# A hybrid decoder layer on one core: another order of the weights' sums and roundings, adding DMAs spread over the taps, tiles kept on chip

## The chip, the core and the metric

The kernel runs on one core of a Trainium2 chip. The metric is the device time of one execution in microseconds (us); it computes one layer for 1024 prompt positions and 8 sample positions, in float32. Engines are named as in the profile: PE is TensorE (PEld its weight loads), DVE VectorE, ACT ScalarE, POOL GpSimd, SP SyncE, which here only issues DMAs.

## What is computed

```python
h = _rmsnorm(x, norm_g)
z = h @ w_in                                   # 1024 -> 6 x 1024
a_val, a_gl, a_gate, b_u, b_v, b_gate = split(z)
a_in = a_val * sigmoid(a_gl)
a_conv = depthwise_conv(concat([conv_buf, a_in]), conv_w) + conv_b     # 31 taps
a_out = silu(layernorm(a_conv, a_ln_g, a_ln_b)) * silu(a_gate)
gated = spatial_gate(layernorm(b_v, ...), w_s, b_s)    # 128x128 causal matrix per head
b_out = b_u * gated * silu(b_gate)
y = x + concat([a_out, b_out]) @ w_out
return rmsnorm(y, final_g), and the new convolution and chunk states
```

## The kernel before

Channels lie on partitions and the 1032 positions along the free dimension, so a [128, 1032] tile holds one block of 128 channels. The large product z = h @ w_in is done by a scheme of Strassen's kind with 7 products in place of 8, and each float32 factor is split into a rounded part and a rest, so that each product is 3 matmuls.

**Units and steps.** `units` is a list of 24 pairs of 128 output columns: P0 to P7 (value and its sigmoid gate, which feed the convolution), v0 to v3 (b_v), B0 to B7 (b_u and its gate), G0 to G3 (the gates of the convolution branch). Steps 0 and 1 do units 0 and 1 together, each step from 2 on does one unit. A step has 7 slots, one for each product of `PRODS`; a slot is 24 matmuls of 258 columns, a step 168. Within a slot the body calls work for the other engines between the two halves of its matmuls, and the order of these calls is the order on every engine's queue.

**Weights.** `wload` (L129) loads a unit's four quarters R1 to R4 from HBM, `wsum` (L140) makes the sums S1 to S4 of quarters on DVE, and `wsplit` (L145) rounds a sum on ACT (H, L154) and subtracts it on DVE (L, L155). Products use quarters 1, 2, 3 and 4 in this order: slots 0 and 1 need H1 and L1, slots 2 and 3 H2 and L2, 4 and 5 H3 and L3, 6 HL4. The order of the calls by slot is written in the loop (L844 to L872). Between slots 0 and 2 ACT copies the first sum of the products to another bank (`zb`, L885), and PE's slot 2 waits for that copy.

**Convolution.** For each P, `conv_items` (L320) puts taps into a queue `fill`: most taps are multiply-adds on DVE (`tap`, L336); the last GTS = 10 taps (none for P7) are products on ACT (`gtap`, L343), which two chains of DMAs issued by POOL add up in SBUF (`accum_op`, L351), and two more adding DMAs add the chains to the result (L365). `pump` (L99) takes items from `fill` for as long as the planner's estimate of DVE's time is less than 1 us ahead of its estimate of PE's.

**LayerNorm of the convolution** (`ln_items`, L371) stands in the same queue behind P7's taps: a mean (matmuls with ones), for each of the 8 blocks a load from DRAM (cD), a subtraction on DVE (`cen`, L398), a square on ACT, a store (ccD), a sum on DVE (`qacc`, L409); then the variance (`var`, L417), a broadcast of 1/std over PE (`ln_bc`, L437), and for each block a reload of ccD and of its gate (sgD), a multiplication (L462), Silu on ACT (L463), a multiplication with the gate (L468) and the split for the output product (`prep_m`, L626). The barrier `bar` holds this last part back until all 24 steps are issued.

**Output product.** 48 groups of 24 matmuls (`mmo`, L644): for each of three groups of positions first 8 output blocks over the gMLP half (half = 1), then 8 over the convolution half (half = 0). The weights of group s are split by `split_w` (L612) two groups ahead.

**Memory.** All of these tiles share one pool of NU = 51 buffers of 4 KB per partition. A new tile takes the buffer that a finished tile gave back and waits for the last instruction or DMA that used it. SP has one queue for all its loads and stores, and `later` delays a store by some slots.

## Time and profile before

| | |
|---|---|
| median of two runs | 878.38 us (878.18 to 878.57) |
| the profiled execution | 876.83 us |
| its span, first to last instruction | 875.0 us, so 1.83 us lie around it |
| mean granted clock of TensorE | 0.936 |
| busy: PE, DVE, ACT, POOL | 768.8, 646.6, 420.5, 82.4 us |
| start (before step 2 begins) | 0 to 97.7 us |
| steps 2 to 23 | 97.7 to 639.2 us |
| output product | 639.2 us to the end |

The digits of the page show tenths of busy time in 40 slices of 21.9 us. A row of the windows gives for one stretch its length, the busy time of each engine with its number of instructions, the granted clock, the DMA engines' share and GB/s. A row of the waits reads: who waited, for whom, us in total, how often, the longest.

### The profile page before, as it was taken

Reading aid. Unit: us, or ns where it says so; the run is one execution under the profiler, and the core shown is the slowest. Engines: PE = TensorE matmul, PEld = TensorE weight load, DVE = VectorE, ACT = ScalarE, POOL = GpSimd, SP = SyncE. Lnnn points to the kernel's source line nnn. Section 1 sums busy time; section 2 is a strip of 40 time slices with the busy share of each in tenths; the row PEclk is TensorE's granted clock in tenths of the full one; section 3 lists DMA queues with packets and bytes.
Section 4 is the critical chain, followed back from the end, with each engine's and each line's share of the span. In section 5 each row is a group of like instructions: output and inputs, shape, how many; then the busy total and the mean of one; then the engine's idle time right before and its main releaser. Section 6 shows DMA issues by size and latency. Waiting matters only on the chain. (4 is left out here: it accounts for less than half of the span.)

```text
span 875.0 us, 13987 instructions
## 1 busy us (share of the span) xinstructions
PE 768.8 (88%) x5648; PEld 751.0 (86%) x5648; DVE 646.6 (74%) x782; ACT 420.5 (48%) x568; POOL 82.4 (9%) x103
## 2 busy tenths in 40 slices
PE   6768998998879998997989999999879499999995
PEld 6767997988869997997989899998879489998994
DVE  4767996977657978878879889996854756725843
ACT  3443563555546575635747654334534434413431
POOL 1010011021130120120211201000010000000000
PEclk7779999999889998998998999999988789999998
DMA  8050178585695595795984977226879723573451
GB/s 297 0 171 16 50 178 202 147 180 148 163 203 178 144 239 149 169 213 153 181 227 97 229 182 200 85 74 230 291 293 413 281 73 121 170 264 105 146 209 51
DMA packets 67512, 151.48 MB, mean 173 GB/s; under 512 B 7448, under 2 KB 28632, under 8 KB 67432
## 3 DMA queue, kind: packets, MB, share of 16 engines
q1 hardware_dynamic: 55352, 106.50, 35.1%
q0 software_dynamic: 12096, 44.10, 26.0%
q8 instruction: 44, 0.72, 0.3%
q14 instruction: 20, 0.16, 0.1%
HBM read 83.58 MB, written 27.55 MB: 127 GB/s over the span
## 5 line engine op out<-in xcount | busy, mean ns | idle before, releaser
L650 PE MATMUL po<-mh,wh 128*128 128x384 f32 (+1 forms) x384 | 126.3, 329 | 19.0 <-ACT wh L616 11.7
L155 DVE TENSOR_TENSOR L<-R,H 128x1024 fp32r<-128x1024 f32 x72 | 87.8, 1220 | 72.0 <-ACT H L154 39.1
L650 PE MATMUL po<-ml,wh 128*128 128x384 f32 (+1 forms) x384 | 124.3, 324 | 0.6 <-DVE ml L641 0.6
L650 PE MATMUL po<-mh,wl 128*128 128x384 f32 (+1 forms) x384 | 124.3, 324 | 0.3 <-DVE wl L618 0.3
L154 ACT ACTIVATE H<-R 128x1024 fp32r<-128x1024 f32 x72 | 74.9, 1053 | 77.2 <-DVE R L142 39.9
L252 PE MATMUL zb<-hT,H 128*128 128x258 f32 x384 | 85.8, 307 | 29.3 <-ACT zb L885 21.4
L339 DVE SCALAR_TENSOR_TENSOR c<-apad,cw,c 128x1024 f32<-128x1024 f32 x85 | 108.6, 1278 | 2.4 <-ACT c L329 2.4
L339 DVE SCALAR_TENSOR_TENSOR accb<-apad,cw,accb 128x1024 f32<-128x1024 f32 x77 | 98.4, 1278 | 0.0
L650 PEld LDWEIGHTS po<-mh,wh 128*128 128x128 f32 x384 | 73.5, 191 | 23.0 <-ACT wh L616 12.0
L347 ACT ACTIVATE prod<-apad,cw 128x1024 f32<-128x1024 f32 x70 | 78.3, 1144 | 29.9 <-DMA prod<-prod 18.6
L252 PEld LDWEIGHTS zb<-hT,H 128*128 128x128 f32 x384 | 64.6, 206 | 32.1 <-ACT zb L885 22.7
L252 PE MATMUL zb<-hnB,HL 128*128 128x258 f32 x384 | 70.7, 299 | 15.1 <-DVE apad L286 11.9
L252 PE MATMUL zb<-lT,H 128*128 128x258 f32 x384 | 82.2, 297 | 0.8 <-DVE lT L238 0.8
L252 PE MATMUL zb<-hT,L 128*128 128x258 f32 x384 | 81.5, 295 | 0.0
L618 DVE TENSOR_TENSOR wl<-wr,wh 128x1024 fp32r<-128x1024 f32 x48 | 58.5, 1223 | 28.3 <-ACT wh L616 28.3
L252 PE MATMUL za<-lnB,H 128*128 128x258 f32 x384 | 77.3, 283 | 0.4 <-DVE lnB L222 0.4
L252 PE MATMUL za<-hnB,H 128*128 128x258 f32 x384 | 77.4, 283 | 0.0
L252 PE MATMUL za<-hnB,L 128*128 128x258 f32 x384 | 77.4, 283 | 0.0
L650 PEld LDWEIGHTS po<-mh,wl 128*128 128x128 f32 x384 | 73.3, 191 | 1.0 <-DVE wl L618 1.0
L650 PEld LDWEIGHTS po<-ml,wh 128*128 128x128 f32 x384 | 73.4, 191 | 0.8 <-DVE ml L641 0.8
L252 PEld LDWEIGHTS zb<-hnB,HL 128*128 128x128 f32 x384 | 58.3, 203 | 17.2 <-DVE apad L286 13.0
L351 POOL DMA_DIRECT2D prod<-prod x56 | 48.4, 864 | 208.3 <-ACT prod L347 109.7
(154 smaller groups left out, 1594.0 us busy)
## 6 DMA issues: line engine op xcount, KB each, us to landing
prod<-prod POOLq DMA_DIRECT2D x56, 512.0 KB, 6.0
R<-w_in SPq DMA_DIRECT2D x96, 256.0 KB, 4.8
wr<-w_out SPq DMA_DIRECT2D x48, 512.0 KB, 5.2
c<-prod POOLq DMA_DIRECT2D x14, 512.0 KB, 5.1
x<-xT SPq DMA_DIRECT2D x8, 516.0 KB, 5.6
sgD<-row SPq DMA_DIRECT2D x8, 516.0 KB, 3.3
mbD<-row SPq DMA_DIRECT2D x8, 516.0 KB, 2.9
ma<-ccD SPq DMA_DIRECT2D x8, 516.0 KB, 10.1
```

The costliest lines, as they stand in the source:

```text
L154: A.activation(h, r, AF.Copy)
L155: V.tensor_tensor(out=l, in0=r, in1=h, op=ALU.subtract)
L252: T.matmul(z[:, s, :PW], lhsT=HL[u, wi][we][:, wh, cs], rhs=F[name, p][xe][:, kt, :], start=first, stop=(kt == 3 and we == 1), skip_group_ ...
L339: V.scalar_tensor_tensor(out=o, in0=ap[:, j:j + NP_], scalar=cw[:, k, j:j + 1], in1=o, op0=ALU.mult, op1=ALU.add)
L347: A.activation(p, ap[:, j:j + NP_], AF.Copy, scale=cw[:, k, j:j + 1])
L351: G.dma_start(st["g", j % 2], p, accum_op=ALU.add)
L618: V.tensor_tensor(out=wl[s], in0=r, in1=wh[s], op=ALU.subtract)
L650: T.matmul(z, lhsT=w[:, cs], rhs=m_[g, half, kt][e], start=(half == 1 and kt == 0 and e == 0 and w is wh[s]), stop=(half == 0 and kt == KT ...
```

## The change

It is one edit in several parts. (1) A unit's R1 is loaded with R4 and R3 in slot 6, one slot earlier than before, and R2 in slot 1 in place of 3. The sums S1 and S3 go to slot 1, S2 to slot 2, S4 to slot 5 of the step before the unit's own; H3 and H4 move from slots 0 and 1 to slots 1 and 2 of its own. (2) GTS is 9 in place of 10, and these products come at every second tap. (3) In the start the squares of the second half of x are summed over blocks by matmuls, 48 in place of 12, and no longer by three additions on DVE. (4) Stores wait one or two slots longer. (5) `delay` items hold mean, variance and broadcast back by 3 to 4 us of estimated time. (6) The centred tiles of blocks 4 to 7 and the gates 6 and 7 stay in SBUF; their stores and reloads go. (7) A head's v is loaded in slot 0 in place of 2, and its normalisation is split between slot 6 and slot 1 of the next step.

```diff
@@ -26,9 +26,11 @@
 CW = 31
 H = CW - 1
 EPS = 1e-6
-GTS = (10,) * 7 + (0,)
+GTS = (9,) * 7 + (0,)
 NU = 51
 MMT = 0.12
+KEEP_C = (4, 5, 6, 7)
+KEEP_G = (6, 7)
 
 
 
@@ -104,6 +106,14 @@
                     return
                 fill.popleft()
                 continue
+            if kind == "delay":
+                if fn is None and margin < 1e8:
+                    fill[0] = (kind, cost, est["pe"] + cost)
+                    return
+                if margin < 1e8 and est["pe"] < fn:
+                    return
+                fill.popleft()
+                continue
             if kind == "pe" and not pe_ok:
                 return
             fill.popleft()
@@ -184,6 +194,13 @@
             for t in range(2):
                 T.matmul(ps[:CN, 0, c:c + 1], lhsT=sq[:, t, c // 3, CN * (c % 3):CN * (c % 3) + CN], rhs=ones_m[:, :1],
                          start=t == 0, stop=t == 1)
+
+    def stat_q(p, q, ps):
+        sq = xsq.pop((p, q))
+        for t in range(2):
+            for c in range(6):
+                T.matmul(ps[:CN, 0, c:c + 1], lhsT=sq[:, t, c // 3, CN * (c % 3):CN * (c % 3) + CN], rhs=ones_m[:, :1],
+                         start=q == 0 and t == 0 and c == 0, stop=q == 3 and t == 1, skip_group_check=True)
 
     def rstd_x(p, ps):
         V.tensor_scalar(out=xrs[:CN, p, :6], in0=ps[:CN, 0, :6], scalar1=EPS, scalar2=None, op0=ALU.add)
@@ -352,8 +369,8 @@
             return f
         for j in range(2, CW - gt):
             fill.append(("dve", 1.2, tap(j)))
-            if j < 2 + gt:
-                fill.append(("dve", 0.0, gtap(CW - gt + j - 2)))
+            if gt and j % 2 == 0 and j < 2 + 2 * gt:
+                fill.append(("dve", 0.0, gtap(CW - gt + j // 2 - 1)))
             if j == 10 and k:
                 acc_item(k - 1)
 
@@ -367,6 +384,7 @@
 
 
     ln = {}
+    mixa = {}
 
     def ln_items():
         acc_item(7)
@@ -388,6 +406,7 @@
             lnload(0)
             lnload(1)
             dve(2.0)
+        fill.append(("delay", 3.0, None))
         fill.append(("pe", 2.0, mean))
 
         def cen(k):
@@ -401,7 +420,10 @@
                 else:
                     ln["s", k] = U([128, NT], f"lns{k}")
                     A.activation(ln["s", k], c, AF.Square)
-                later(lambda: SP.dma_start(ccD[k], lnc.pop(k)), 1)
+                if k in KEEP_C:
+                    mixa[k] = c
+                else:
+                    later(lambda: SP.dma_start(ccD[k], lnc.pop(k)), 2)
             return f
 
         def qacc(k):
@@ -425,7 +447,9 @@
             G.tensor_tensor(out=rs[:, 1, :8], in0=rs[:, 0, :8], in1=nhalf[:, :8], op=ALU.pow)
             G.tensor_tensor(out=rs[:NS, 1, 8:9], in0=rs[:NS, 0, 8:9], in1=nhalf[:NS, :1], op=ALU.pow)
             ln["v"] = True
+        fill.append(("delay", 3.0, None))
         fill.append(("pe", 2.0, var))
+        fill.append(("delay", 4.0, None))
         fill.append(("bar", 0.0, None))
         fill.append(("pe", 2.5, ln_bc))
         for k in range(8):
@@ -448,15 +472,15 @@
         for k in range(3):
             mixa_load(k)
 
-    mixa = {}
-
     def mixa_load(k):
         while outq:
             slot_end()
-        mixa[k] = U([128, NT], f"ma{k}")
-        SP.dma_start(mixa[k], ccD[k])
-        ln["g", k] = U([128, NT], f"sg{k}")
-        SP.dma_start(ln["g", k], sgD[k])
+        if k not in KEEP_C:
+            mixa[k] = U([128, NT], f"ma{k}")
+            SP.dma_start(mixa[k], ccD[k])
+        if k not in KEEP_G:
+            ln["g", k] = U([128, NT], f"sg{k}")
+            SP.dma_start(ln["g", k], sgD[k])
 
     def mixa_norm(k):
         V.tensor_tensor(out=mixa[k], in0=mixa[k], in1=ln["r"], op=ALU.mult)
@@ -578,7 +602,7 @@
             V.memset(r1[:, :H], 0.0)
             V.tensor_tensor(out=r1[:, H:], in0=r1[:, H:], in1=r0, op=ALU.mult)
             dve(1.25)
-            later(lambda: SP.dma_start(csT[128 * k:128 * k + 128, :], r1[:, NP_:]), 1)
+            later(lambda: SP.dma_start(csT[128 * k:128 * k + 128, :], r1[:, NP_:]), 3)
             conv_items(k, r1)
             if k == 7:
                 ln_items()
@@ -589,10 +613,13 @@
             V.tensor_tensor(out=r1, in0=r1, in1=t2.pop(k), op=ALU.mult)
             V.tensor_tensor(out=r1, in0=r1, in1=r0, op=ALU.mult)
             dve(2.3)
-            later(lambda: SP.dma_start(mbD[k], r1), 1)
+            later(lambda: SP.dma_start(mbD[k], r1), 3)
             return []
-        later(lambda: SP.dma_start(sgD[2 * k], r0), 1)
-        later(lambda: SP.dma_start(sgD[2 * k + 1], r1), 1)
+        for e, r in enumerate((r0, r1)):
+            if 2 * k + e in KEEP_G:
+                ln["g", 2 * k + e] = r
+            else:
+                later(lambda e=e, r=r: SP.dma_start(sgD[2 * k + e], r), 2)
         return []
 
 
@@ -786,6 +813,8 @@
         scale_x(0, 3)
         xform(0, "nT3")
 
+        xst = []
+
         def start_x(si, slot):
 
             if si == 0:
@@ -795,22 +824,26 @@
                         wsum(u, "S2")
                         wsplit(u, 2)
                 if slot == 1:
+                    for q in range(2):
+                        square_x(1, q)
                     xform(0, "nB21")
-                    for q in range(4):
+                    for q in range(2, 4):
                         square_x(1, q)
+                    xst.append(PS("e", "xst1"))
                 if slot == 2:
+                    stat_q(1, 0, xst[0])
+                    stat_q(1, 1, xst[0])
                     xform(0, "T1")
                     for u in range(2):
                         wsplit(u, 3)
-                    sum_x(1)
                 if slot == 3:
+                    stat_q(1, 2, xst[0])
+                    stat_q(1, 3, xst[0])
+                    rstd_x(1, xst.pop())
                     xform(0, "nT4")
                     for u in range(2):
                         wsum(u, "S4")
                         wsplit(u, 4)
-                    p = PS("e", "xst1")
-                    stat_x(1, p)
-                    rstd_x(1, p)
                 if slot == 4:
                     bcast_x(1, PS("e", "xbc1"))
                     xform(0, "nB22")
@@ -846,29 +879,27 @@
                 if slot in (0, 1):
                     Z[bank] = PS(bank, f"z{bank}{si}")
 
-                if own and slot == 0:
-                    wsum(u, "S4")
+                if si and own and slot == 1:
                     wsplit(u, 3)
-                if own and slot == 1:
+                if si and own and slot == 2:
                     wsplit(u, 4)
                 if nxt is not None:
-                    if slot == 0:
-                        wload(nxt, 1)
-                    elif slot == 2:
+                    if slot == 1:
                         wsum(nxt, "S1")
-                    elif slot == 3:
                         wsum(nxt, "S3")
                         wload(nxt, 2)
+                    elif slot == 2:
+                        wsum(nxt, "S2")
                     elif slot == 4:
                         wsplit(nxt, 1)
                     elif slot == 5:
-                        wsum(nxt, "S2")
+                        wsum(nxt, "S4")
                     elif slot == 6:
                         wsplit(nxt, 2)
-                if slot == 6 and (own or si == 1) or (si == 0 and slot == 6):
+                if slot == 6:
                     n2 = 2 if si == 0 else u + 2 if own else 3
                     if n2 < N_U:
-                        for i in (4, 3):
+                        for i in (4, 3, 1):
                             wload(n2, i)
                 prod(slot, lanes, range(0, 2))
                 if slot == 0 and prev:
@@ -919,12 +950,13 @@
 
                 if own and si + 1 < len(steps) and units[u + 1][0] == "B":
                     h = units[u + 1][1]
-                    if slot == 2:
+                    if slot == (2 if h == 0 else 0):
                         v_load(h)
-                    if slot in (5, 6):
-                        v_norm(h, range(4 * (slot - 5), 4 * (slot - 5) + 4))
+                    if slot == 6:
+                        v_norm(h, range(0, 4))
                 if kind == "B" and own:
                     if slot == 1:
+                        v_norm(k, range(4, 8))
                         gw = gate_work(k)
                     if slot in (3, 4):
                         gw.pop(0)()
```

Three places show what the new order is. The first is ACT around the start of step 6 (unit 6): H6_1 to HL6_4 are the roundings of that unit's quarters, prod1 the products for the adding DMAs of P1, zb6 the copy that PE's slot 2 waits for. Before:

```order
L154 ACTIVATE H6_1_1772<-R6_1_1634 128x1024
L347 ACTIVATE prod1_28_1802<-apad1_487,cw_76 128x1024
L347 ACTIVATE prod1_29_1819<-apad1_487,cw_76 128x1024
L154 ACTIVATE H6_2_1839<-R6_2_1736 128x1024
L347 ACTIVATE prod1_30_1871<-apad1_487,cw_76 128x1024
L154 ACTIVATE H6_3_1877<-R6_3_1599 128x1024
L282 ACTIVATE row0_5_1766<-zb5_1663 128x2x258
L885 ACTIVATE zb6_1910<-za6_1875 128x2x258
L154 ACTIVATE HL6_4_1914<-R6_4_1597 128x512
```

and in the changed kernel:

```order
L164 ACTIVATE H6_1_1790<-R6_1_1627 128x1024
L364 ACTIVATE prod1_25_1834<-apad1_520,cw_76 128x1024
L164 ACTIVATE H6_2_1851<-R6_2_1696 128x1024
L299 ACTIVATE row0_5_1784<-zb5_1684 128x2x258
L364 ACTIVATE prod1_26_1902<-apad1_520,cw_76 128x1024
L916 ACTIVATE zb6_1921<-za6_1886 128x2x258
L164 ACTIVATE H6_3_1925<-R6_3_1625 128x1024
L920 ACTIVATE p7_6_1957<-ze6_1924 128x516
L364 ACTIVATE prod1_27_1959<-apad1_520,cw_76 128x1024
L164 ACTIVATE HL6_4_1963<-R6_4_1623 128x512
```

The copy zb6 stands ahead of H6_3 now, and two products of taps where three stood.

The second is SP at the same place, the loads of units 7 and 8 (R8_1 is quarter 1 of unit 8). Before:

```order
L135 DMA R8_4_2109<-w_in 128x512
L135 DMA R8_3_2111<-w_in 128x512
L500 DMA cv_p<-va2_1_1897 128x256
L502 DMA vD2_119<-va2_0_1896 128x1024
L502 DMA vD2_119<-va2_1_1897 128x1024
L135 DMA R8_1_2146<-w_in 128x512
L135 DMA R8_2_2249<-w_in 128x512
```

and in the changed kernel:

```order
L145 DMA R8_4_2128<-w_in 128x512
L145 DMA R8_3_2130<-w_in 128x512
L145 DMA R8_1_2132<-w_in 128x512
L524 DMA cv_p<-va2_1_1901 128x256
L526 DMA vD2_119<-va2_0_1900 128x1024
L526 DMA vD2_119<-va2_1_1901 128x1024
L145 DMA R8_2_2200<-w_in 128x512
```

R8_1 no longer stands behind the stores.

The third is DVE between the splits of the output weights wl1 and wl8, while PE does the first eight groups of the output product. Before, from wl1 to the second of the final multiplications (ma):

```order
L618 TENSOR_TENSOR wl1_6416<-wr1_6277,wh1_6414 128x1024
L618 TENSOR_TENSOR wl2_6432<-wr2_6388,wh2_6430 128x1024
L409 TENSOR_TENSOR lnq_6030<-lnq_6030,lns7_6311 128x1032
L618 TENSOR_TENSOR wl3_6463<-wr3_6428,wh3_6461 128x1024
L423 TENSOR_SCALAR rs_84<-lnv_6474 128x8
L424 TENSOR_SCALAR rs_84<-lnv_6474 8x1
L462 TENSOR_TENSOR ma0_6502<-ma0_6502,lnr_6488 128x1032
L618 TENSOR_TENSOR wl4_6540<-wr4_6459,wh4_6538 128x1024
L462 TENSOR_TENSOR ma1_6506<-ma1_6506,lnr_6488 128x1032
```

and in the changed kernel, from wl7 to the variance:

```order
L645 TENSOR_TENSOR wl7_6578<-wr7_6538,wh7_6576 128x1024
L431 TENSOR_TENSOR lnq_6408<-lnq_6408,lns2_6488 128x1032
L417 TENSOR_TENSOR lc4_6485<-lc4_6485,lnmean_6400 128x1032
L431 TENSOR_TENSOR lnq_6408<-lnq_6408,lns3_6556 128x1032
L417 TENSOR_TENSOR lc5_6553<-lc5_6553,lnmean_6400 128x1032
L431 TENSOR_TENSOR lnq_6408<-lnq_6408,lns4_6593 128x1032
L417 TENSOR_TENSOR lc6_6590<-lc6_6590,lnmean_6400 128x1032
L431 TENSOR_TENSOR lnq_6408<-lnq_6408,lns5_6597 128x1032
L417 TENSOR_TENSOR c7_5553<-c7_5553,lnmean_6400 128x1032
L431 TENSOR_TENSOR lnq_6408<-lnq_6408,lns6_6601 128x1032
L431 TENSOR_TENSOR lnq_6408<-lnq_6408,lns7_6605 128x1032
L445 TENSOR_SCALAR rs_84<-lnv_6609 128x8
```

Before, one sum (lnq) of the LayerNorm's squares was left behind wl1; now all eight centrings (lc, and c7 for block 7) and seven sums stand between wl2 and the variance (rs), which itself stands behind wl7. On PE the variance's matmuls stood in group 1 behind its fifth block of channels, and now in group 5 at the same place.

## The prediction

> **What bounds the kernel now.** I read the windows by stage first, then who PE waited for, then the engines that it waited for.
>
> ```profile
> 0.00:97.70 97.70, 74.06 (x496) 70.48 (x497) 65.77 (x90) 42.51 (x55) 4.96 (x11) 0.83 0.33 113
> 97.70:526.90 429.20, 385.89 (x3043) 379.56 (x3042) 351.91 (x419) 243.34 (x325) 69.70 (x83) 0.95 0.74 175
> 526.90:591.90 65.00, 65.00 (x541) 64.69 (x541) 64.30 (x67) 24.85 (x41) 2.26 (x3) 1.00 0.40 117
> 591.90:639.20 47.30, 43.12 (x345) 41.39 (x343) 34.26 (x35) 24.13 (x33) 0.00 (x0) 1.00 0.78 279
> 639.20:700.30 61.10, 42.67 (x231) 41.14 (x229) 35.44 (x39) 25.33 (x31) 2.19 (x2) 0.81 0.86 324
> ```
>
> The columns are length, busy time of PE, PEld, DVE, ACT and POOL, granted clock, DMA share, GB/s. The rows are the start, steps 2 to 18, steps 19 to 21, steps 22 and 23, and the first eight groups of the output product. The third row is the yardstick: three steps in 65.00 us with PE busy throughout at full clock, 21.67 us a step. POOL is nearly idle there, since the last adding DMAs of the convolution are over. At that pace the 17 steps of the second row would take 368.4 us; they take 429.2. So 60.8 us are lost: 43.3 with PE idle (429.20 - 385.89), the other 17.5 mostly by the lower clock. Steps 19 to 21 hold two heads' gate matmuls; the 17 hold six, and the four v units' transposes, so the share of such extras is alike. For PE's idle time there:
>
> ```profile
> PE zb L252 <- ACT zb L885: 21.4, 6, 5.0
> PE zb L252 <- DVE apad L286: 11.9, 5, 5.8
> PE vp L483 <- ACT p L889: 2.4, 1, 2.4
> PE zb L252 <- DVE row L286: 2.3, 2, 1.5
> PE vps L492 <- ACT va L485: 2.0, 1, 2.0
> PE gs L563 <- DVE t L554: 1.9, 2, 1.4
> PE zb L252 <- ACT zc L893: 1.1, 1, 1.1
> ```
>
> Half is PE at slot 2, waiting for ACT's copy L885; the next is PE waiting for DVE to empty a bank. ACT and DVE in turn, in the same stretch:
>
> ```profile
> DVE L L155 <- ACT H L154: 30.9, 14, 6.2
> ...
> DVE R L142 <- DMA R<-w_in: 3.4, 3, 1.9
> ...
> ACT H L154 <- DVE R L142: 21.0, 10, 4.8
> ACT prod L347 <- DMA prod<-prod: 18.6, 8, 6.1
> ACT H L154 <- DMA prod<-prod: 16.5, 8, 5.5
> ...
> ACT vh L540 <- DMA vh<-vD: 11.1, 2, 9.3
> ACT vsn L523 <- DVE rs L520: 8.9, 1, 8.9
> ```
>
> ACT waits for DVE's sums, DVE for ACT's roundings, both for buffers that adding DMAs still hold (prod<-prod), and all stands on ACT's queue ahead of the copy. One case, on ACT and then PE in step 6:
>
> ```profile
> 197.70 1.06 ACT L154 ACTIVATE H<-R 128x1024 fp32r<-128x1024 f32 x1 [6.80 <-issue]
> 199.92 0.80 PE L252 MATMUL zb<-hT,H 128*128 128x258 f32 x2 [5.01 <-ACT zb L885]
> ```
>
> **Steps 2 to 21: the gain.** In the new order H3 stands behind the copy, and H1, H2 and H4 follow sums that DVE made one to two slots earlier, so ACT no longer meets a sum that is not there. The adds:
>
> ```profile
> 188.32 0.85 POOL L351 DMA_DIRECT2D prod<-prod  x1 [1.85 <-DMA prod<-prod]
> 191.62 0.86 POOL L351 DMA_DIRECT2D prod<-prod  x1 [2.45 <-DMA prod<-prod]
> ```
>
> ```profile
> L339 DVE SCALAR_TENSOR_TENSOR c<-apad,cw,c 128x1024 f32<-128x1024 f32 x85 | 108.6, 1278 | 2.4 <-ACT c L329 2.4
> ...
> prod<-prod POOLq DMA_DIRECT2D x56, 512.0 KB, 6.0
> R<-w_in SPq DMA_DIRECT2D x96, 256.0 KB, 4.8
> ...
> ma<-ccD SPq DMA_DIRECT2D x8, 516.0 KB, 10.1
> ```
>
> An add lands 6.0 us after its issue, and two chains alternate, so one can start each 3 us; before they came 3.3 us apart (188.32, 191.62) and each waited for one before it. With a product at every second tap and some 8 taps in a step of 21.67 us, they come about 5.4 us apart: the queue stays empty and a product's buffer is free again some 7 us after it was written. So I take away: of the 21.4 us at the copy 15.5 (the wait at step 8 stays, since there ACT stands at L523, which the change leaves; half of the small ones); of PE's waits for DVE's emptying, 11.9 + 2.3, about two thirds, 9, since they come when DVE has fallen behind by its own waits for H, of which those for a missing sum go and those for a buffer shrink; of the other 7.4 likewise 5. That is 29.5 of 43.3, or 68%, and with the same share of the 17.5 us of clock 41.5 us. Against it stand seven more taps on DVE: 7 x 1.278 = 8.9 us. PE's work hides them: with 8 more, DVE would be busy 360 of some 388 us, 93%, and the third row ran at 64.30 of 65.00 without holding PE up. I take off 1.5 us: -40. Bounds: -15 if only PE's waits at the copy go with nothing of the clock, -58 if the 17 steps come to the pace of the yardstick but for the wait at L523.
>
> **The start.** Three additions on DVE go, and 36 more small matmuls come:
>
> ```profile
> 52.90 3.65 PE L185 MATMUL xst<-ones_m,xsq 128*86 128x1 f32 x24 [6.31 <-DVE xsq L178]
> ```
>
> ```profile
> 52.90:59.60 6.70, 6.70 (x39) 6.70 (x40) 4.20 (x6) 2.33 (x3) 0.00 (x0) 0.50 0.90 307
> ```
>
> Before, PE idled 6.31 us and then took 3.65 us for 12 matmuls (24 records) at half clock. 48 of them take 14.6 us at half clock and not less than 7.3 at full; without the idle time the clock stays up, so 7.3 to 9 in place of 9.96, and some 1.6 us less at half clock after it: -3, with -5 and +5 (half clock stays) as bounds.
>
> **Steps 22 and 23.** The LayerNorm's centring leaves them, and ten of P7's taps come in; PE idled 4.2 us of 47.30 there: -2 (-4 to +2).
>
> **The output product's first groups: the loss.** What leaves steps 22 and 23 is late next here. The LayerNorm must be over before the convolution half can start, and before all but one of its sums ran under steps 22 and 23. These rows are the chain before:
>
> ```profile
> L618 DVE TENSOR_TENSOR wl<-wr,wh 128x1024 fp32r<-128x1024 f32 x9 | 11.0, 1224 | 11.7 <-ACT wh L616 11.7
> ...
> L409 DVE TENSOR_TENSOR lnq<-lnq,lns 128x1032 f32<-128x1032 f32 x1 | 1.2, 1226 | 0.0
> ```
>
> ```profile
> 652.24 0.14 DVE L424 TENSOR_SCALAR rs<-lnv 8x1 f32<-8x1 f32 x1
> 660.02 1.23 DVE L462 TENSOR_TENSOR ma<-ma,lnr 128x1032 f32<-128x1032 f32 x1 [7.64 <-ACT lnr L447]
> ...
> 690.57 1.23 DVE L462 TENSOR_TENSOR ma<-ma,lnr 128x1032 f32<-128x1032 f32 x1
> ...
> 694.00 1.23 DVE L462 TENSOR_TENSOR ma<-ma,lnr 128x1032 f32<-128x1032 f32 x1
> ```
>
> ```profile
> 701.53 0.69 PE L650 MATMUL po<-mh,wl 128*128 128x384 f32 x1 [0.25 <-DVE wl L618]
> ...
> 708.78 8.69 PE po L650 x48
> ```
>
> Before, the convolution half got going 701.53 - 639.2 = 62.3 us after the output product's start. Now: DVE has seven splits (7 x 1.22), fifteen centrings and sums (15 x 1.23) and two splits of the gMLP half (some 1 us each) ahead of the variance, 29 us. PE gets there after 5.6 groups of 4.35 us and the mean, 27 us. The DMAs move seven weights, seven reloads and four stores of half a MB, 9.4 MB, 29 us at the 324 GB/s of that row. Three chains of equal length that wait for each other: I take 34 us (29 if they overlap fully, 42 if DVE meets waits as the 11.7 us before). From there rs to the first multiplication as before, 7.8; seven blocks at 694.00 - 690.57 = 3.43, 24.0; from the last to the start 7.5. Sum 73.3, or +11 (+6 to +19). PE has only 2.4 groups, 10 us, to do behind the variance, so nearly all of the 39 us of that tail is seen; the delay items cost nothing of their own, since the same queue is emptied in group 5. The twelve transfers that tiles kept on chip save are hidden: in the old chain no multiplication waited for a reload.
>
> **The sum.** -40 - 3 - 2 + 11 = -34 us on the profiled execution's 876.83 us: 842.8. The median lies 1.55 us above that execution: 844 us.
>
> **Rivals.** First, the buffers stay late: 51 are as few as before, H and L still take those that adds gave back, and 63 of 70 products remain. Steps 2 to 18 then give back only some 12 us: 872 us. For it speak 16.5 and 18.6 us of waits on adds; against it, that these came in bunches of ten.
>
> An add's issue could also wait for DVE: then a denser DVE makes all adds late and steps 2 to 18 keep their 60.8 us, 876.83 - 3 - 2 + 11 + 1.55 = 884 us. The rows speak against it:
>
> ```profile
> 187.38 1.28 DVE L339 SCALAR_TENSOR_TENSOR accb<-apad,cw,accb 128x1024 f32<-128x1024 f32 x1
> ...
> 245.77 1.23 DVE L155 TENSOR_TENSOR L<-R,H 128x1024 fp32r<-128x1024 f32 x1 [11.77 <-DMA prod<-prod]
> ```
>
> ```profile
> 235.54 0.84 POOL L351 DMA_DIRECT2D prod<-prod  x1 [9.09 <-ACT prod L347]
> ```
>
> At 188.32 DVE was in its tap and POOL's issue took 0.85 us; at 235.54 DVE stood idle (its 11.77 us) and it took 0.84. The Trainium skill (SBUF — State Buffer, "SBUF: two separate sides") states that GpSimd writes the descriptors of such DMAs and is locked out while VectorE holds the port pair that they share. By that rule this rival would be the likely one; the trace does not agree.
>
> The slower one: the loads of R1 come too late. R1 is asked for in slot 6, third of three loads, and its sums stand in slot 1, about two slots (6.2 us) later, where before it had three. At the 4.8 us of the row nothing waits. If these loads land as late as the reloads did under load, 10.1 us, DVE waits 3.9 us in each of 21 steps, 0.6 of it covered by DVE's slack (21.67 - 21.1): +69, 913 us. It eats the gain from a landing of some 8.4 us on. Against it: DVE waited for such a load 3.4 us in all.
>
> The better one: every step comes to the yardstick's pace and the three chains overlap, -55 - 3 - 3 + 6: 823 us.
>
> **How the numbers follow.** Forecast 0.52, better 0.18, late buffers 0.18, adds behind DVE 0.05, late loads 0.07. A measurement of this kernel can tell about 2%, 861 to 896 us, from no change. Faster: the forecast nearly whole, the better case and a tail of the late buffers, 0.74; same 0.19; slower 0.07. The range, 818 to 868 us, goes from a little below the better case to near the late buffers.
>
> **What would show it.** In the new profile: PE's waits for L885's successor under 8 us; DVE's waits for H under 12; no clock of 0.5 in the steps but around step 8; a step at some 22.5 us; the convolution half starting about 73 us after the output product, with PE idle some 20 us ahead of it. It is wrong if the waits on prod<-prod stay above 30 us, or if DVE waits for R from w_in in most steps.

## The result, and the profile after

The changed kernel takes 846.5 us (median of two runs, 846.36 to 846.64) against 878.38: a ratio of 0.964, 95% interval 0.960 to 0.968. The forecast was 844.0. Its profiled execution took 846.36 us, with a span of 844.0 against 875.0. The windows of the changed kernel, cut at the same places as those of before (length, then busy time of PE, PEld, DVE, ACT and POOL, granted clock, DMA share, GB/s):

```profile
0.00:99.40 99.40, 83.38 (x569) 80.32 (x570) 63.20 (x88) 41.34 (x54) 5.98 (x11) 0.79 0.31 113
99.40:482.30 382.90, 370.47 (x3043) 366.72 (x3042) 345.74 (x413) 228.92 (x311) 59.40 (x71) 0.99 0.73 175
482.30:548.30 66.00, 65.36 (x543) 64.83 (x542) 61.99 (x66) 31.27 (x47) 6.52 (x8) 1.00 0.68 180
548.30:588.60 40.30, 40.30 (x339) 40.30 (x338) 35.08 (x35) 15.33 (x23) 0.00 (x0) 1.00 0.55 184
588.60:669.60 81.00, 44.24 (x236) 41.58 (x234) 51.00 (x51) 34.71 (x41) 2.19 (x2) 0.78 0.64 234
```

Read against the five rows of before: the start +1.7 us, steps 2 to 18 -46.3, steps 19 to 21 +1.0, steps 22 and 23 -7.0, the first eight groups of the output product +19.9; the rest went from 174.7 to 174.4. The sum is -31.0. So the steps gave more than forecast and the end took more back. The start's +1.7 us is not to be read as a loss: kernels with the same form of the start differ by as much (98.1 to 100.1 us in five that have the new form, 96.0 to 99.6 in eight that have the old one; the table below).

The waits of PE, DVE and ACT in steps 2 to 18 of the changed kernel, the rows that answer to those of before:

```profile
PE zb L269 <- ACT zb L916: 4.5, 1, 4.5
...
DVE L L165 <- ACT H L164: 23.3, 17, 4.0
DVE R L152 <- DMA R<-w_in: 0.4, 1, 0.4
...
ACT H L164 <- DMA prod<-prod: 8.9, 4, 4.0
...
ACT prod L364 <- DMA c<-prod: 6.4, 2, 3.3
...
ACT HL L164 <- DMA c<-prod: 5.2, 1, 5.2
ACT prod L364 <- DMA prod<-prod: 3.8, 3, 2.6
```

PE waits for the copy once (21.4 us in six times before), in step 8. Of ACT's waits for buffers that adds hold, the two rows that the prediction showed fell from 35.1 us (18.6 + 16.5) to 12.7 (8.9 + 3.8); with the adds at a channel tile's end (c<-prod) and all smaller rows it is 54.6 before and 27.7 now. ACT's 21.0 us of waits for DVE's sums have no row any more. DVE's waits for H went only from 30.9 to 23.3.

The LayerNorm's end in the changed kernel, in order of time (start, duration, what; in brackets the idle time before and its releaser):

```profile
629.93 3.70 PE L443 MATMUL lnv<-ones_m,lnq 128*128 128x1 f32 x18 [13.71 <-DVE lnq L431]
633.67 0.17 DVE L445 TENSOR_SCALAR rs<-lnv 128x8 f32<-128x8 f32 x1 [3.79 <-PE lnv L443]
641.32 2.38 DVE L486 TENSOR_TENSOR ma<-ma,lnr 128x1032 f32<-128x1032 f32 x2 [7.43 <-ACT lnr L471]
663.41 1.23 DVE L486 TENSOR_TENSOR c<-c,lnr 128x1032 f32<-128x1032 f32 x1
669.63 0.69 PE L677 MATMUL po<-mh,wh 128*128 128x384 f32 x1 [18.39 <-ACT wh L643]
```

PE stands idle twice, 13.71 us until DVE has the last sum of squares, and 18.39 us until the first weights of the convolution half are rounded, behind the eight blocks on ACT's queue. The first of these gaps was not there before.

### The profile page after: what moved, and what is told of

Same layout as the page of the kernel before. It is cut to its first block, busy times and chain, and to the rows that moved or that the text cites. A ratio compares the mean times of both kernels' runs of the same rounds, so it can differ in the third digit from the quotient of the medians.

```text
span 844.0 us, 14083 instructions
## 1 busy us (share of the span) xinstructions
PE 761.8 (90%) x5720; PEld 747.5 (89%) x5720; DVE 652.0 (77%) x786; ACT 412.0 (49%) x561; POOL 77.4 (9%) x96
## 3 DMA queue, kind: packets, MB, share of 16 engines
q0 software_dynamic: 11088, 40.43, 24.8%
## 4 chain that ended last, share of the span: by engine, by line
PE 51%; DVE 11%; DMA 5%; ACT 4%; issue 3%; POOL 0%; SPq 0%; DVEq 0%; ACTq 0%; POOLq 0%
PE po L677 18%; PE zb L269 13%; PE za L269 9%; PE ze L269 4%; PE zc L269 4%; DVE c L356 1%; PE gp L576 1%; DMA c<-prod 1%; DMA wc<-wcD 1%; DMA prod<-prod 1%; DVE accb L356 1%; DVE lnq L431 1%; DVE L L165 1%; DVE yt L689 1%; DVE wl L645 1%
## 5 line engine op out<-in xcount | busy, mean ns | idle before, releaser
L677 PE MATMUL po<-mh,wh 128*128 128x384 f32 (+1 forms) x384 | 125.3, 326 | 25.7 <-ACT wh L643 18.4
L356 DVE SCALAR_TENSOR_TENSOR accb<-apad,cw,accb 128x1024 f32<-128x1024 f32 x84 | 107.4, 1278 | 0.0
L269 PE MATMUL zb<-hT,H 128*128 128x258 f32 x384 | 82.3, 296 | 10.2 <-ACT zb L916 4.5
L364 ACT ACTIVATE prod<-apad,cw 128x1024 f32<-128x1024 f32 x63 | 71.9, 1144 | 22.4 <-DMA prod<-prod 7.2
L269 PE MATMUL zb<-lT,H 128*128 128x258 f32 x384 | 80.0, 291 | 0.5 <-DVE lT L255 0.5
L269 PEld LDWEIGHTS zb<-hT,H 128*128 128x128 f32 x384 | 62.1, 198 | 11.5 <-ACT H L164 4.8
L269 PE MATMUL zb<-hnB,HL 128*128 128x258 f32 x384 | 66.5, 285 | 4.8 <-DVE row L303 2.7
L368 POOL DMA_DIRECT2D prod<-prod x49 | 42.3, 863 | 281.4 <-ACT prod L364 234.1
L269 PEld LDWEIGHTS zb<-lT,H 128*128 128x128 f32 x384 | 62.1, 198 | 0.7 <-DVE lT L255 0.7
```

Source lines behind the costliest of these rows:

```text
L269: T.matmul(z[:, s, :PW], lhsT=HL[u, wi][we][:, wh, cs], rhs=F[name, p][xe][:, kt, :], start=first, stop=(kt == 3 and we == 1), skip_group_ ...
L356: V.scalar_tensor_tensor(out=o, in0=ap[:, j:j + NP_], scalar=cw[:, k, j:j + 1], in1=o, op0=ALU.mult, op1=ALU.add)
L364: A.activation(p, ap[:, j:j + NP_], AF.Copy, scale=cw[:, k, j:j + 1])
L368: G.dma_start(st["g", j % 2], p, accum_op=ALU.add)
L677: T.matmul(z, lhsT=w[:, cs], rhs=m_[g, half, kt][e], start=(half == 1 and kt == 0 and e == 0 and w is wh[s]), stop=(half == 0 and kt == KT ...
```

## The experiments

Two pairs of explanations had to be told apart: what made the steps faster (the order of sums and roundings, or the buffers of the adds), and why the end got longer. All spans and stages are of each run's profiled execution, medians of its timed runs; a stage is cut as above. In the two rows with early weights the last cut lies inside the convolution half's first matmuls, so there only the sum of the last two stages can be compared.

| kernel | start | 2-18 | 19-21 | 22-23 | eight groups | rest | median |
|---|---|---|---|---|---|---|---|
| before | 97.7 | 429.1 | 65.1 | 47.3 | 61.1 | 174.8 | 878.4 |
| changed | 99.4 | 382.9 | 66.0 | 40.3 | 81.0 | 174.4 | 846.5 |
| before + order | 97.5 | 404.3 | 65.1 | 50.9 | 64.0 | 175.1 | 858.1 |
| before + spread adds | 98.2 | 380.1 | 66.8 | 51.3 | 64.5 | 174.6 | 837.9 |
| before + both | 96.0 | 381.9 | 65.2 | 44.0 | 79.8 | 175.8 | 845.6 |
| changed, nothing kept | 98.2 | 382.4 | 65.1 | 40.3 | 86.2 | 174.1 | 850.1 |
| changed, old order | 100.1 | 387.8 | 65.5 | 45.7 | 63.0 | 175.7 | 838.2 |
| changed, tap cost 1.13 | 98.4 | 381.0 | 65.2 | 43.6 | 72.5 | 175.6 | 837.2 |
| before + third chain | 99.6 | 444.7 | 65.1 | 47.3 | 61.1 | 174.5 | 894.5 |
| spread, adds held | 99.5 | 393.2 | 65.1 | 52.0 | 65.3 | 175.1 | 852.2 |
| spread + P7 | 98.5 | 378.3 | 66.9 | 47.2 | 61.3 | 174.4 | 830.9 |
| changed + P7 and early weights | 98.1 | 381.0 | 65.6 | 56.0 | 49.1 | 176.9 | 827.6 |
| spread + P7 and early weights | 97.7 | 378.7 | 67.0 | 48.7 | 50.1 | 176.3 | 819.2 |
| changed, wide sums in the start | 96.4 | 380.0 | 65.5 | 40.4 | 81.1 | 174.5 | 840.7 |

**The order alone.**

```diff
-                if own and slot == 0:
-                    wsum(u, "S4")
+                if own and slot == 1:
                     wsplit(u, 3)
-                if own and slot == 1:
+                if own and slot == 2:
                     wsplit(u, 4)
...
-                        for i in (4, 3):
+                        for i in (4, 3, 1):
```

(with the sums' and loads' slots of the change; the rest as before)

> The kernel before with only the new order of the weights' sums, roundings and loads; the adding DMAs stay bunched, ten products a channel tile. Theory O (the order is what counts: no rounding on ACT stands ahead of the copy for PE any more, and DVE makes the sums a slot or two earlier): steps 2 to 23 fall from 541.5 us to some 505, two thirds or more of the 52 us that the whole change takes from them; median near 840 to 848, since the LayerNorm stays under the steps. Theory B (what counts is the buffers that bunched adding DMAs hold): steps 2 to 23 stay above 525 us, ACT and DVE still wait more than 30 us for prod<-prod, median 862 or more.

858.07 us, ratio 0.976 (0.973 to 0.980): between the two. Steps 2 to 23 took 520.3 us, so 21 of the 52 us are gained. Steps 2 to 18 of this kernel, and PE's and ACT's waits there:

```profile
97.50:501.81 404.31, 376.53 (x3043) 370.93 (x3041) 346.03 (x413) 240.10 (x322) 68.83 (x82) 0.98 0.78 185
...
PE zb L252 <- DVE apad L286: 6.7, 4, 3.2
PE gs L563 <- DVE t L554: 6.5, 3, 3.3
PE zb L252 <- ACT zb L883: 5.0, 2, 4.0
...
ACT prod L347 <- DMA prod<-prod: 8.1, 6, 3.3
ACT H L154 <- DMA prod<-prod: 7.7, 4, 3.2
```

Most of the waits at the copy are gone, as theory O says (21.4 to 5.0), and yet about half of what the change gains in steps 2 to 18 is missing: PE still waits for DVE (6.7 + 6.5 us in these two rows, 11.9 + 1.9 before), and ACT and DVE still wait for adds.

**The spreading alone.**

```diff
-GTS = (10,) * 7 + (0,)
+GTS = (9,) * 7 + (0,)
...
-            if j < 2 + gt:
-                fill.append(("dve", 0.0, gtap(CW - gt + j - 2)))
+            if gt and j % 2 == 0 and j < 2 + 2 * gt:
+                fill.append(("dve", 0.0, gtap(CW - gt + j // 2 - 1)))
```

> The kernel before with only nine products in place of ten and one at every second tap; the order of the weights' sums is the old one. Theory B: steps 2 to 23 fall to 507 us or less, median near 845. Theory O: PE's waits for the copy of Z at slot 2 stay above 14 us of their 21.4, ACT still waits for R's sums, steps 2 to 23 above 523 us, median 862 or more. In both the waits for prod<-prod fall below 25 us.

837.93 us, ratio 0.954 (0.950 to 0.957): theory B, and faster than the whole change. The edit does two things, nine products in place of ten and one at every second tap; no run tries them apart. Its steps 2 to 18, and the waits there:

```profile
98.17:478.23 380.06, 370.60 (x3043) 366.88 (x3042) 353.03 (x420) 232.41 (x314) 61.94 (x74) 0.99 0.76 183
...
PE zb L252 <- ACT zb L885: 6.4, 2, 6.1
...
ACT H L154 <- DVE R L142: 19.2, 9, 4.3
...
ACT prod L347 <- DMA prod<-prod: 8.2, 3, 3.3
```

ACT still waits 19.2 us for sums that are not there, against 21.0 before, and it costs PE next to nothing: the copy comes in time in all steps but two. These waits, which my working counted among the causes, seem to do harm only on top of the waits for buffers.

**Both together, and nothing else.**

> The kernel before with the order and the spreading together, and nothing else of the change (old start, old stores, no tiles kept on chip, no delay items, v tiles loaded and normalised as before). If the two make the gain: steps 2 to 23 at 489 to 494 us as in the changed kernel, median 840 to 850, with the LayerNorm's tail again long if it comes from the gain itself (the taps end later against PE), or 62 us as before if the tail is the delay items' doing, and then the median is near 828. If other parts carry more than 5 us of the steps (later stores, the v tiles), steps 2 to 23 come out above 495 us.

845.59 us, ratio 0.962 (0.958 to 0.966): the time of the whole change, stage by stage within 4 us. Start, stores, kept tiles, delay items and the v tiles together are worth nothing beside these two. Order and spreading do not add up in steps 2 to 18: 24.8 and 49.0 us alone, 47.2 together. And the long end is here without any delay item: with steps 22 and 23 it is 123.8 us, while the spreading alone has 115.8.

**The old order put back into the changed kernel.** The second edit that asks for the same, from the other side.

> The changed kernel with the old order of the weights' sums, roundings and loads; spread adds, start, stores, kept tiles and delay items as changed. Theory P (spread adds alone carry steps 2 to 18; the new order only makes the planner put the taps later, so that the LayerNorm comes late): steps 2 to 18 at 380 to 385 us as in the changed kernel, the last tap at least 25 us ahead of the output product (11.6 us in the changed kernel), steps 22 and 23 with the first eight groups 5 us or more under their 121.3 us, median 836 to 842. Rival (the new order is needed beside the other parts, and the difference between 837.9 and 845.6 us came from elsewhere): steps 2 to 18 above 390 us, median above 846.

838.16 us, ratio 0.951 (0.947 to 0.956): 8.3 us faster than the changed kernel, as theory P says, though steps 2 to 18 at 387.8 us are 3 us over its band. (This run and the next stood beside a kernel before of 881.25 us; by the ratios they gain a little more.) The old order loses 10 us in the steps and wins 18 in the eight groups. What moved is seen at the mean's matmuls (count, duration, first and last start), here in the changed kernel:

```profile
L400 PE MATMUL lnm<-ssum,ones_m x4: 592/592/592, 591.7 to 593.0; 128*128 128x512 f32 x4
```

and here with the old order:

```profile
L400 PE MATMUL lnm<-ssum,ones_m x4: 592/592/593, 573.6 to 574.9; 128*128 128x512 f32 x4
```

The mean comes 3.1 us after the output product's start (588.6) in the one, 25.5 us ahead of it (599.1) in the other. Counted in the traces, 162 of the 169 taps are done by the end of step 21 with the old order and 154 with the new one: the items stand in the same order, but the planner, which meets the sums' estimates in other slots, lets some 0.4 taps less into each step. The mean's place is not all of it: in the run with order and spreading alone it stands 12.1 us ahead of the output product, and yet the variance (`rs`) comes 43.4 us after it, against 45.1 in the changed kernel and 27.8 with the old order. In these runs it goes with how many of the eight subtractions are done before the output product begins: none in the changed kernel, two in that run, six with the old order.

**One number of the planner.**

```diff
-            fill.append(("dve", 1.2, tap(j)))
+            fill.append(("dve", 1.13, tap(j)))
```

> The changed kernel with one number changed: the planner's cost of a tap is 1.13 us in place of 1.2, so that it puts about half a tap more into each step; the work is the same. Theory P: the last tap is issued about a step earlier, the LayerNorm's mean stands ahead of the output product, steps 22 and 23 with the first eight groups fall from 121.3 to 105 to 115 us, steps 2 to 21 stay at 449 us plus 0 to 3, median 836 to 842. Rival (DVE itself is at its limit in the steps, so that the taps can't come earlier): steps 2 to 21 grow by 5 us or more, what the end gains the steps lose, median 845 to 850.

837.18 us, ratio 0.950 (0.947 to 0.953): theory P. Steps 2 to 21 took 446.3 us (448.9 in the changed kernel), so DVE had room for the taps, and steps 22 and 23 with the eight groups fell from 121.3 to 116.0 us, just short of the band of 105 to 115. The mean now stands 13.4 us ahead of the output product:

```profile
L400 PE MATMUL lnm<-ssum,ones_m x4: 592/592/592, 574.8 to 576.1; 128*128 128x512 f32 x4
```

**Buffers or ACT's queue?** The spreading changes two things: fewer products wait in buffers, and products no longer stand in bunches ahead of ACT's copies. Two runs move the first and leave the order of work on ACT as it is (in the traces ACT's instructions follow each other in the same order as in the kernel that each starts from). A third chain, first:

```diff
-                if j < CW - gt + 2:
-                    st["g", j % 2] = p
+                if j < CW - gt + 3:
+                    st["g", j % 3] = p
                 else:
-                    G.dma_start(st["g", j % 2], p, accum_op=ALU.add)
+                    G.dma_start(st["g", j % 3], p, accum_op=ALU.add)
```

> The kernel before with three chains of adding DMAs in place of two (ten products as before, bunched as before, and one more add at a channel tile's end): ACT's bunches are the same, but adds can start each 2 us in place of 3. Theory B (PE's lost time comes from buffers that waiting adds hold): ACT's waits for prod<-prod, 35 us before, fall below 20, and steps 2 to 18 fall from 429 to 415 us or less, median 866 or less. Rival (bunching hurts because ten products stand on ACT's queue ahead of the copies for PE): steps 2 to 18 stay above 423 us, median 872 to 880.

894.52 us, 13 us slower than the kernel before beside it (881.25; ratio 1.015, 1.012 to 1.018): both expectations missed. More chains hardly drained the bunch faster: adds with more of them under way landed later (6.0 us before), two landings never came closer than 2.42 us (2.46 before), and a third add to the same result came at a tile's end:

```profile
prod<-prod POOLq DMA_DIRECT2D x49, 512.0 KB, 7.4
...
ACT prod L347 <- DMA prod<-prod: 24.2, 9, 6.3
ACT prod L347 <- DMA c<-prod: 18.7, 6, 5.5
```

So more buffers were held, and longer (a third chain is itself one more buffer): all of ACT's waits in steps 2 to 18 for such adds, the rows with prod<-prod and c<-prod summed, rose from 54.6 to 68.0 us, and with ACT's bunches unchanged these steps took 15.6 us more. This reading was made after the result. The other way round, from the spread kernel:

```diff
+                    held.append((j, p))
+                while len(held) > 3 or (j == CW - 1 and held):
+                    i, q = held.pop(0)
+                    G.dma_start(st["g", i % 2], q, accum_op=ALU.add)
```

> The kernel before with the spreading (its own run: 837.9 us, steps 2 to 18 in 380.1), but each add is issued three products late, so that three products more stand in buffers at any time; ACT's queue is that of the spread kernel, instruction for instruction. Theory B (bunched adds cost time because products that wait for them hold buffers): waits for prod<-prod on ACT and DVE come back, steps 2 to 18 lose a third or more of their gain, 396 us or more, median 850 or more. Rival (bunched products cost time because they stand on ACT's queue ahead of the copies for PE): steps 2 to 18 stay at 378 to 386 us, median 836 to 843.

852.21 us, ratio 0.970 (0.965 to 0.975). Steps 2 to 18 took 393.2 us, 13.1 of the 49.0 us lost again: between the bands, nearer to theory B's. ACT's waits for such adds rose from 17.3 to 23.5 us. The largest case, on ACT and then on PE:

```profile
210.51 1.15 ACT L347 ACTIVATE prod<-apad,cw 128x1024 f32<-128x1024 f32 x1 [5.33 <-DMA prod<-prod]
211.57 1.06 ACT L489 ACTIVATE va<-vp 128x512 f32<-128x512 f32 x2
```

```profile
212.69 0.59 PE L496 MATMUL vps<-ident,row 128*8 128x128 f32 x2 [6.02 <-ACT va L489]
```

These 6.0 us, and a stretch of 6.8 us at clock 0.50 around them (209.4 to 216.2 us) that the spread kernel does not have, make some 9 of the 13.1 us, by my estimate (6.0 and half of 6.8). Another 2.5 us of PE's idle time, at 268.9 us, follow on a load that DVE waited 8.1 us for, and not on an add. The loss is thus a few events and not many small ones.

DVE waits for such buffers too. This is its row for them in steps 2 to 18, first before, then with three chains, with the adds held back and in the spread kernel:

```profile
DVE L L155 <- DMA prod<-prod: 13.9, 2, 11.8
...
DVE L L155 <- DMA prod<-prod: 15.9, 3, 5.8
...
DVE L L155 <- DMA prod<-prod: 5.3, 3, 3.5
...
DVE L L155 <- DMA prod<-prod: 1.1, 1, 1.1
```

Counting a product as alive from ACT's write to the landing of the DMA that used it up, steps 2 to 18 hold on average 3.03 products in the spread kernel (at most 5), 3.20 with the adds held back, 3.53 before (at most 8), 4.23 with three chains. Their times are 380.1, 393.2, 429.1 and 444.7 us, in the same order. So with ACT's work in the same order, holding more buffers cost time in both pairs. The new order alone has 3.48 alive and 404.3 us: it is a second remedy, with which ACT meets 22.5 us of these waits in place of 54.6 though as many products are alive, and it has little left to do beside the spreading. The sum of ACT's waits is no measure of the loss by itself: the changed kernel, with 2.95 alive, has 27.7 us of them and steps of 382.9 us. How the 49 us divide between held buffers, ACT's bunches and the tenth product stays open: no run had as many buffers held as before with the products spread.

**Nothing kept on chip.**

```diff
-KEEP_C = (4, 5, 6, 7)
-KEEP_G = (6, 7)
+KEEP_C = ()
+KEEP_G = ()
```

> The changed kernel with no convolution tile and no gate kept on chip: four more stores and six more loads. By the prediction these transfers are hidden: within 1.5 us of the changed kernel, 845 to 848. Rival: in the output product's first eight groups the DMAs are the bound (0.86 of them busy before), then 3 MB more at 324 GB/s cost up to 9.7 us: 851 to 856.

(The edit brings back six stores and six loads; the expectation counts two stores too few.) 850.05 us, ratio 0.968 (0.965 to 0.971), 3.6 us over the changed kernel, though the two intervals overlap; the eight groups took 5.1 us more. That part is seen in the trace: without the kept gates the last gates' stores stand ahead of the first reload on SP's queue, and the first subtraction waits, where in the changed kernel it waited for no DMA:

```profile
597.94 1.23 DVE L417 TENSOR_TENSOR lc<-lc,lnmean 128x1032 f32<-128x1032 f32 x1 [5.91 <-DMA lc<-cD]
```

**A shorter end.** Three runs try to have the gain of the steps without the loss behind them. First P7, whose taps end last, gets nine products too (two additions on DVE take them up), and the Activation that ACT meets too early in step 8 goes two slots later:

```diff
+GTS = (9,) * 8
...
+                if k == 7:
+                    V.tensor_tensor(out=c[:, :NP_], in0=c[:, :NP_], in1=g, op=ALU.add)
```

> The kernel before with the spreading (its own run: 837.9 us), the last channel tile with nine products too, their two sums added by DVE, and the sampled rows' normalisation on ACT moved two slots later. Theory P: nine taps less and two sums more take 9 us from DVE, the LayerNorm's sums stand under steps 22 and 23 again, the variance comes 20 us earlier, the stretch from step 22 to the convolution half falls from 115.8 to 90 to 100 us; the wait of 6.1 us in step 8 goes with the half clock behind it, another 5 to 8 us: median 810 to 822. Rival (DVE and ACT only swap waits: the normalisation chain is bound by its own 3.4 us a block and starts no earlier): 830 or more.

830.91 us, ratio 0.943 (0.936 to 0.950): in the rival's band, though not for the rival's reason, since the chain did start earlier. The variance's matmuls came 8 us after the output product's start in place of 26, but the stretch from step 22 to the convolution half fell only from 115.8 to 108.5: the blocks, once they could start early, were placed between PE's groups and went at their pace, and PE still ended on the weights' rounding:

```profile
PE po L656 <- ACT wh L622: 11.9, 1, 11.9
```

Two slots were too few for step 8: the wait stayed at 5.6 us. Then the convolution half's first two weights are rounded and split ahead of the last blocks (the output weights are loaded two groups earlier for it), these two groups' matmuls go block by block in turn, and the Activation of step 8 moves four slots; once from the spread kernel, once from the changed one (there with a tap's cost at 1.06 and no delay items):

```diff
+                    if nt == 5:
+                        for e in range(8, 10):
+                            split_w(e)
...
+            if s == 8:
+                for kt in range(7):
+                    mmo(8, range(kt, kt + 1))
+                    mmo(9, range(kt, kt + 1))
```

> The kernel before with the spreading and the last channel tile's products (its own run: 830.9 us), and the later normalisation of the sampled rows and the two early weights as in the run with the new order. Against that run: the wait of 5.6 us at step 8 goes and the half clock behind it, 5 to 8 us; the 11.9 us in which PE stood idle ahead of the convolution half are filled, 9 to 15 us: median 808 to 817. Rival (the early weights' roundings only push the blocks back by as much): 820 or more.

819.2 us, ratio 0.932 (0.927 to 0.938): the fastest here, 27 us under the changed kernel. The eight groups and the rest took 226.4 us, 9.3 less than in the run with nine products for P7, since the 11.9 us that PE waited ahead of the convolution half shrank to pieces:

```profile
PE po L661 <- ACT mh L651: 3.5, 2, 1.8
PE po L661 <- DVE yt L673: 2.5, 1, 2.5
```

Step 8 gave nothing: its 5.6 us became 2.6 there, for a split, and 2.7 in step 9, for a head's sample rows (the units stand mixed in the list: step 8 is G0, step 9 B0), and steps 2 to 18 stayed at 378.7. The median was 2 us over its band, and just under the rival's 820.

The same from the changed kernel:

> The changed kernel, with the new order, and: a tap's planned cost 1.06 us, no delay items, nine products for the last channel tile too, the sampled rows' normalisation on ACT two thirds of a step later, and the convolution half's first two weights rounded and split ahead of the last normalisation blocks, with these two groups' matmuls taken in turn by block. Theory P: the LayerNorm's variance comes about 25 us earlier than in the changed kernel, PE no longer idles for the first weights' rounding, the wait of 4.5 us in step 8 goes with its half clock: median 800 to 815. Rival (DVE is at its limit in the steps with the denser taps): steps 2 to 21 grow by more than 8 us over 449, median above 820.

827.64 us, ratio 0.942 (0.937 to 0.947). Steps 2 to 21 did not grow (446.6), but steps 22 and 23 did, from 40.3 to 56.0: with the new order the last tile's sums came as PE stood at the mean:

```profile
PE lnm L403 <- DVE ssum L326: 4.6, 1, 4.6
```

It missed its band by 13 us, without the sign that its rival had named. In each of the three pairs tried the old order with spread adds came out some 8 us faster: this one, in which the change's smaller parts differ too, the spread kernel without and with the new order, and the changed kernel with and without it.

**The start.** The 48 small matmuls over the squares move one column each. This run moves 64 equal ones:

```diff
-                T.matmul(ps[:CN, 0, c:c + 1], ..., rhs=ones_m[:, :1], ...
+                T.matmul(ps[:CN, 0, 64 * c:64 * c + 64], ..., rhs=ones_m[:, :64], ...
```

> The changed kernel, with 64 equal columns in place of one in each of the start's 48 small matmuls over the squares; the sums read one column of each 64. Theory C (matmuls of one column leave the array almost idle, so the clock is granted as if PE had paused): the two stretches of clock 0.5 between 46 and 63 us go or shrink to one slice of 3.4 us, although the matmuls move 64 times the columns, and the start takes 96 to 98.5 us in place of 99.4. Rival (the halved clock there comes from something else, such as ACT's or DVE's late work): the same two stretches at 0.5, and a start of 99 to 104 us, since the matmuls are longer. Both: the rest as in the changed kernel, median 843 to 850.

840.67 us, ratio 0.956 (0.954 to 0.959): theory C, with a median under the 843 to 850 that both named. In the changed kernel the stretch of these matmuls, and DVE at its end, look so:

```profile
46.30:53.10 6.80, 6.80 (x38) 6.80 (x37) 2.69 (x3) 2.32 (x3) 0.00 (x0) 0.50 0.00 0
53.10:56.50 3.40, 3.40 (x46) 3.40 (x45) 0.00 (x0) 0.66 (x2) 0.00 (x0) 1.00 0.00 0
56.50:63.30 6.80, 6.80 (x36) 6.80 (x36) 3.99 (x6) 1.70 (x2) 3.41 (x2) 0.50 0.59 197
```

```profile
57.48 0.16 DVE L206 TENSOR_SCALAR xrs<-xst 86x6 f32<-86x6 f32 x1 [8.50 <-PE xst L202]
```

and with 64 columns:

```profile
46.90:53.70 6.80, 6.80 (x78) 6.80 (x76) 2.03 (x2) 2.33 (x4) 0.00 (x0) 1.00 0.57 165
```

```profile
54.05 0.16 DVE L208 TENSOR_SCALAR xrs<-xst 86x6 f32<-86x6 f32 x1 [5.12 <-PE xst L202]
```

PE is busy without a pause in both, by its own records, and with one column it gets the half clock. The four other kernels with this start show the same: in all five, 10.3 to 13.6 us between 43 and 64 us at clock 0.50, and none in the run with 64 columns, whose next half clock comes at 63.9 us, behind a stretch of 3.40 us in which PE was busy for 1.10. With 64 times the columns the sums are ready 3.4 us earlier, and the start takes 96.4 us, 1.7 under the fastest of those five. Steps 2 to 18 were 2.9 us shorter too, for which no part of this edit is a reason.

## Why the prediction was right or wrong

The time was right to 2.5 us, but by luck in part: the sum (-34, measured -31.0) came out because its errors cancelled. The steps gave 10.3 us more than forecast (5.3 in steps 2 to 21, 5.0 in 22 and 23), the output product's groups took 8.9 more back, and the start missed by 4.7.

**Steps 2 to 21: -40, measured -45.3.** The place of the loss and its size were right; the sum was a little short. PE's idle time fell by 30.9 us (43.3 to 382.90 - 370.47 = 12.4; I had 29.5), what the clock had lost by 15.4 of 17.5 (I had 12), and the 1.5 us for seven more taps did not show in steps 2 to 18; steps 19 to 21, which the sum took as unchanged, took 1.0 us more. The cause was half right. I had named two, the order ("H3 stands behind the copy ... so ACT no longer meets a sum that is not there") and the spread adds, and summed their gain without dividing it; the one place that prices the order without the buffers is the rival of late buffers, at some 12 us. Alone, the order gave 24.8 us and the spreading 49.0. The spreading does it all, with the sums still missing; the order adds nothing to it and costs some 8 us at the end, which no step of my working saw. The rival of late buffers fell: fewer products are alive (2.95 on average, 3.53 before) though the pool is as small.

**Steps 22 and 23: -2, measured -7.0.** PE was busy for all of the 40.30 us, so its 4.2 us of idle time went. The other 2.8 us are for the most part work of PE that moved and was not saved: the mean's matmuls, four of 592 ns, now stand behind the output product's start, where PE's busy time rose from 42.67 to 44.24 us. My sum had no term for that.

**The output product's first groups: +11, measured +19.9.** The chain was right, its first term mis-sized. I took 34 us to the variance, between 29 and 42; `rs` came at 45.1 (633.67 - 588.6), over the upper bound, and so the stage is just over its own bound of +19. Behind it the forecast stood: 7.65 us to the first multiplication (7.8), 22.1 to the last (24.0), 6.2 to the start (7.5), so 36.0 in place of 39.3. (The 7.5 was counted to the matmul at 701.53; the half's first one stands at 700.27 in the trace of before, which makes it 6.3.) The waits of DVE and ACT in the stretch to the variance:

```profile
DVE wl L645 <- ACT wh L643: 10.9, 5, 2.6
...
ACT lns L422 <- DVE lc L417: 13.5, 6, 3.6
```

DVE's split waits for ACT's rounding, which stands on ACT's queue behind a square, which waits for DVE's subtraction: two engines in step with each other. Up to its last sum DVE was busy for 27.8 us, about the 29 that I had counted; these 10.9 us and some 2.6 of other waits make it 41.3. The variance's own matmuls, 3.8 us until `rs` could start, were not in the sum at all. The upper bound was the likelier value, as the row of before (11.7 us of the same wait) had said.

"The twelve transfers that tiles kept on chip save are hidden" was wrong by up to 5.1 us: before, the reloads came under the steps; in the run with nothing kept they came with the last gates' stores ahead of them. That the delay items cost nothing was not tried by itself; the run with order and spreading, without them, took 123.8 us from step 22 to the convolution half, against 121.3.

**The start: -3, measured +1.7.** The +1.7 lies within what starts of the same form differ by, so the -3 did not come, and a loss is not shown. "without the idle time the clock stays up" failed: PE had no idle time at these matmuls, and the clock went to a half twice. With 64 columns the start took 96.4 us, 1.3 under the 97.7 of before; kernels with the old start took 96.0 to 99.6. The Trainium skill (TensorE: Matmul & The Clock Gate, Part 1: The HAM clock gate) says that the gate follows how busy PE has been of late; the records of these one-column matmuls, busy 6.80 of 6.80 us at 0.50, show that busy in the profile is not what the gate counted here.

**The other rivals.** Late loads: DVE waited 0.4 us for R. Adds behind DVE: POOL's issues took 863 ns each, 864 before, with DVE busier (90% of steps 2 to 18, 82% before):

```profile
L368 POOL DMA_DIRECT2D prod<-prod x49 | 42.3, 863 | 281.4 <-ACT prod L364 234.1 <-DMA prod<-prod 32.5 <-DVE accb L356 7.8
```

The lock that I had weighed from the Trainium skill (SBUF — State Buffer, "SBUF: two separate sides") is not seen here: in the kernels before and after no issue of such an add took over 1.1 us. That section has GpSimd locked out of writing descriptors while VectorE runs an operation in a two-port mode; I had taken it for every operation of DVE, so the rule, as it stands there, did not make this rival the likely one.

**The signs named ahead.** Met: the copy (4.5 us, under 8), half clock in the steps only at step 8, 22.5 us a step, PE idle some 20 us ahead of the convolution half (18.4); the waits on prod<-prod stayed under 30 us (16.1 on ACT, none on DVE). Missed: that half began after 81.0 us and not 73; and DVE waited 23.3 us for H, not under 12. This last sign was badly chosen: DVE has 37 us to spare in these steps, and PE waited only 5.0 us for it.

## What to carry to other kernels

Where a queue stalls on buffers, find who holds them longest: spacing out the producers, one product for every second tap, gave more here than a reordering of the queue that stood behind them, and the two did not add up. After a gain in one stage, read what was hidden under that stage by the planner's placing; work that is counted in estimates moves with every edit that touches the estimates, and a single constant (1.2 to 1.13) was worth some 9 us here. When two engines hand each other pieces in turn, count their waits from a row of the same pair, not their work alone.

## What the runs showed of the hardware

Matmuls of one column do not keep the clock up, though PE shows no pause: in the changed kernel the granted clock was 0.50 for 6.80 us in their midst and again from their end on, and four more kernels with them had 10.3 to 13.6 us of it at the same place; with 64 columns each they ran at 1.00. Adding DMAs gain little from more chains: with three chains in place of two those of 512 KB landed after 7.4 us in place of 6.0, with no two landings closer than 2.42 us (2.46 with two), and the whole became slower.
